# A Strassen-like product for six up-projection groups, channels in quarters, and another order of the seven products

## The chip, the cores and the metric

One core of one Trainium2 chip. The metric is the device time of one execution in microseconds, the median of several runs. The kernel before: 1018.52 us, median of 3 runs (1018.37 to 1019.42).

## The reference

One decoder layer over 512 positions and 1024 channels, in float32: a normalised input goes through one wide projection into four branches (two kinds of linear attention, softmax attention with forgetting, a gated recurrence), which are projected back, weighted by sigmoid gates and summed. Then comes a squared-ReLU channel mixer. The parts that the change touches:

```
z = h @ w_in + b_in                      # its last 4096 columns are the gates
g = sigmoid(gates)
merged = sum(g * (ycat @ w_branch))
x = x + merged @ w_o
h2 = rms_norm(x, norm2_g)                # 512 x 1024
x = x + square(relu(h2 @ w_up)) @ w_down # w_up 1024 x 4096, w_down 4096 x 1024
```

## The kernel before

All large products run on TensorE in float32r with each operand split into a high part (a cast) and a low part (the rest), and three matmuls high·high, high·low and low·high per tile. The unit of work is a `Group` (line 273): 512 output columns of a weight matrix against all 512 positions, four PSUM banks of 512 columns each. With 1024 rows of weights it is 8 x 4 x 3 = 96 matmuls of 512 columns.

Weights come through four raw buffers of 512 KB (line 198), loaded by SP's queue in the order of a plan (`pull`, line 204); a buffer is given back (`give`, line 218) by the step that reads it last, and the next load is issued then. `exact` (line 226) makes a piece out of a raw buffer: ScalarE casts the high part (L229), VectorE subtracts it for the low part (L230). Four such pairs of buffers exist (line 86), so a piece's cast waits until the matmuls of the piece four before it are done. `split(i)` is called three pieces ahead of the product in hand.

`Seven` (line 337) is the other unit. It does the same work as a 96-matmul group by one level of a Strassen-Winograd scheme: the weights are cut into quarters w11, w12, w22, w21 of 512 rows by 256 columns, the input into four quarters, and seven products of half size replace eight. Its pieces p0 to p6 are sums of quarters made by VectorE (the sum of two raw quarters at L360, L364, L368 and L376, then `exact`). Each product is 2 x 4 x 3 = 24 matmuls of 256 columns (L411), 168 in a seven. The products add up in three PSUM banks Y, Z and X; partial sums of Y are copied out by ScalarE between products (L415, in halves, and L419), because later products go on adding in the same bank, and VectorE makes the output quarters (L420, L425, L432). `forms(f)` gives the input's side of a product: a plain quarter or one of four sums, which `combos` (line 1012) makes once, with VectorE and ScalarE. `spare` are two half buffers for the sum that p0 and p4 need.

Of the eight gate groups six are sevens; each is followed by a branch projection, a `Group` of 48 matmuls. The channel mixer does not use `Seven`: two halves of 2048 channels, each four up groups (`up_group`, line 1127; ReLU on ScalarE L1136, square on VectorE L1138, cast on ScalarE L1139, low part on VectorE L1140) and two down groups over these 2048 channels (`down_group`, line 1148; 192 matmuls each, evacuated by VectorE at L1151, which adds into x).

The order of instructions on each engine is made by a scheduler at build time, from the order in the program as priority and from modelled readiness. It also moves instructions between groups: a matmul of the following group can be placed before the last products of a seven. Steps of other work are generators in `gens`, advanced by `pump()` between products.

Of the kernel before, what the change touches and what calls it, by code (L numbers as in the profile page):

```python
# [76 lines left out]
def tile_hybrid(ctx, tc, x, norm1_g, w_in, b_in, ml_norm_g, fx_qnorm_g, fx_knorm_g, lru_conv_w,  # L77
# [37 lines left out]
    def f32(ap):  # L115
        return ap.bitcast(F32)
# [109 lines left out]
    def exact(pc, raw, off=0):  # L226
        halves_tiles(pc, off)
        hi, lo = pc["hl"]
        nc.scalar.copy(hi, raw)  # L229
        nc.vector.tensor_sub(lo, raw, f32(hi))  # L230
# [106 lines left out]
    class Seven:  # L337
# [11 lines left out]
        def plan(self):  # L349
            w11, w12, w22, w21 = lds = [dict(src=s) for s in self.src]  # L350
            loads.extend(lds)
            me = {}

            def take():
                me["e"] = spare[0]
                spare.append(spare.pop(0))
                return me["e"]

            def p0(pc):
                nc.vector.tensor_add(take(), w11["raw"], w12["raw"])  # L360
                exact(pc, w11["raw"], WOFF)

            def p1(pc):
                nc.vector.tensor_add(w11["raw"], me["e"], w22["raw"])  # L364
                exact(pc, me["e"], WOFF)

            def p2(pc):
                nc.vector.tensor_add(w12["raw"], w12["raw"], w22["raw"])  # L368
                exact(pc, w11["raw"], WOFF)

            def p3(pc):
                exact(pc, w12["raw"], WOFF)
                give(w12)

            def p4(pc):
                nc.vector.tensor_add(me["e"], w11["raw"], w21["raw"])  # L376
                exact(pc, w21["raw"], WOFF)
                give(w11, w21)

            def p5(pc):  # L380
                exact(pc, me["e"], WOFF)

            def p6(pc):
                exact(pc, w22["raw"], WOFF)
                give(w22)

            pieces.extend(dict(make=m) for m in (p0, p1, p2, p3, p4, p5, p6))

        def run(self):
            p0 = piece_no[0]  # L390
            piece_no[0] += 7
            Y, Z, X = acc(), acc(), acc()
            y2, z2, x2 = (t.rearrange("p (b c) -> p b c", c=256) for t in (Y, Z, X))
            s1, u2 = w2(), w2()
            seen = set()
            for f, ps in enumerate((Y, Z, Y, Y, X, Y, Z)):
                split(p0 + f + 3)
                whi, wlo = (kview(t, 4) for t in pieces[p0 + f]["hl"])
                ahi, alo = self.forms(f)
                fresh = id(ps) not in seen  # L400
                seen.add(id(ps))
                for b in range(2):
                    o = ps[:, b * 256 : (b + 1) * 256]
                    bs = slice(b * P, (b + 1) * P)
                    for k in range(4):
                        s0 = fresh and b == 0 and k == 0
                        trio = ((whi, ahi), (whi, alo), (wlo, ahi))
                        for n, (w_, a_) in enumerate(trio):
                            fl = dict(start=s0 and n == 0, stop=k == 3 and n == 2, skip_group_check=True)
                            if self.fm:  # L410
                                nc.tensor.matmul(o, w_[:, k, bs], a_[:, k], **fl)  # L411
                            else:
                                nc.tensor.matmul(o, a_[:, k, bs], w_[:, k], **fl)
                    if f in (0, 2):
                        nc.scalar.copy((s1 if f == 0 else u2)[:, b * 256 : (b + 1) * 256], o)  # L415
                    pump()
                if f == 3:
                    d = self.dst(1, 1)
                    nc.scalar.copy(d, y2)  # L419
                    nc.vector.tensor_sub(d, z2, d)  # L420
                    self.post(1, 1, d)
                    pump()
                elif f == 4:
                    d = self.dst(0, 0)
                    nc.vector.tensor_add(d, x2, s1.rearrange("p (b c) -> p b c", c=256))  # L425
                    self.post(0, 0, d)
                elif f == 5:
                    self.post(1, 0, y2)
                    pump()
                elif f == 6:  # L430
                    d = self.dst(0, 1)
                    nc.vector.tensor_sub(d, z2, u2.rearrange("p (b c) -> p b c", c=256))  # L432
                    self.post(0, 1, d)
# [575 lines left out]

    S = {}  # L1010

    def combos(quarter, give_back):

        qs = [slots.get(), slots.get()]
        t11, t12, t21, t22 = (kview(t[:, o : o + 1024], 4) for t in qs for o in (0, 1024))
        for t, (i, j) in ((t21, (1, 0)), (t22, (1, 1)), (t11, (0, 0)), (t12, (0, 1))):
            nc.vector.tensor_add(t, *(f32(a) for a in quarter(i, j)))
# [10 lines left out]
        out(1, t22)  # L1028
        yield
        nc.vector.tensor_sub(t21, t11, t21)  # L1030
        out(3, t21)
        yield
        nc.vector.tensor_sub(t11, t22, t11)
        out(2, t11)
        yield
        nc.vector.tensor_add(t12, t12, t11)
        out(6, t12)
        slots.free(*qs)
        yield

    def h_quarter(i, j):
        return tuple(k4(t[j], 4)[:, :, i * 256 : (i + 1) * 256] for t in (hTh, hTl))

    def h_forms(f):
        return S[f] if f in S else h_quarter(*{0: (0, 0), 4: (0, 1), 5: (1, 1)}[f])

    def gate_seven(n, half):
        def dst(i, j):
# [75 lines left out]

    Rh, Rl = [None] * 4, [None] * 4

    def up_group(g):
        q = g % 4

        def pre():  # L1130
            Rh[q], Rl[q] = slots.get(F32R), slots.get(F32R)
# [13 lines left out]
            lambda k: xgl[k // 4][:, (k % 4) * 512 : (k % 4 + 1) * 512], evac, pre=pre,  # L1145
        )

    def down_group(fh, ch):
        def evac(tb, ps):
            a = xt(tb)[:, ch * 512 : (ch + 1) * 512]  # L1150
            nc.vector.scalar_tensor_tensor(a, ps, r2[:, tb : tb + 1], a, op0=ALU.mult, op1=ALU.add)  # L1151
            if fh == 1:
                nc.scalar.dma_start(out[tb * P : (tb + 1) * P, ch * 512 : (ch + 1) * 512], a)

        return Group(
            w_down[fh * 2048 : (fh + 1) * 2048], ch * 512, 4, False,
            lambda k: Rh[k // 4][:, (k % 4) * 512 : (k % 4 + 1) * 512],
            lambda k: Rl[k // 4][:, (k % 4) * 512 : (k % 4 + 1) * 512], evac,
        )

    ups, downs = [], []
    for fh in range(2):
        ups.append([up_group(fh * 4 + i) for i in range(4)])
        downs.append([down_group(fh, ch) for ch in range(2)])


    plan = [g_fq, g_fk, g_fv, g_gqk, g_gv, g_mq, g_mk, g_gg, g_mv, g_mo, g_rx, g_ry]
    for _, _, a_, b_ in merge_groups:
        plan += [a_, b_]
    plan += og  # L1170
    for fh in range(2):
        plan += ups[fh] + downs[fh]
    for g in plan:
        g.plan()

# [162 lines left out]
    for i, (n, half, gg_, pg_) in enumerate(merge_groups):  # L1338
# [12 lines left out]
            prep(n)  # L1351
        if n == order[-1] and half == 1:
            slots.free(*hTh, *hTl, *s_slots)
        if n == order[0] and half == 1:
            room = slots.get()
            spare.extend((room[:, :1024], room[:, 1024:2048]))
            s_slots.append(room)
# [13 lines left out]
    og[0].run()  # L1371
    og[1].run()
    slots.free(gains, *mh, *ml_)
    for fh in range(2):
        for g in ups[fh]:
            g.run()
        if fh == 0:
            nc.vector.tensor_scalar(r2, r2, 1.0 / D, EPS, op0=ALU.mult, op1=ALU.add)
            nc.vector.reciprocal(r2, r2)
        else:  # L1380
            slots.free(*xgh, *xgl)
        for g in downs[fh]:
            g.run()
        slots.free(*Rh, *Rl)


_INS = ("x", "norm1_g", "w_in", "b_in", "ml_norm_g", "fx_qnorm_g", "fx_knorm_g", "lru_conv_w", "lru_conv_b",
# [22 lines left out]
```

## Time and profile before

| | before |
|---|---|
| median of 3 runs | 1018.52 us |
| the profiled execution | 1018.88 us |
| its span, first to last instruction | 1017.1 us |
| TensorE matmul busy | 1004.4 us (99%) |
| TensorE weight loads busy | 831.2 us (82%) |
| VectorE busy | 561.0 us (55%) |
| ScalarE busy | 414.0 us (41%) |

Matmuls overlap their neighbours in the trace, so the duration of one (about 390 ns for 512 columns) is not its cost; the distance between two starts is. Times in rows of the timeline and the chain count from the span's first instruction.

### The profile page before, as it was taken

To read this page: it belongs to the slowest core of one execution; us is meant where nothing else is said; L and a number is where in the kernel's file an instruction comes from. 1 tells how busy PE (TensorE), PEld (TensorE's weight loads), DVE (VectorE), ACT (ScalarE), POOL (GpSimd) and SP (SyncE) were. 2 spreads that over 40 slices of the span, in tenths; PEclk is the share of its full clock that TensorE was granted. 3 is DMA by queue.
4 is the path that set the end of the run, shared out by engine and by line. 5 is a ranking of instruction groups with operands and counts; after the bars stand their busy time and mean duration, and the time that the engine had idled before them with its cause. 6 is when DMAs were issued, how large, how long until landed. Compare 5 with 4: busy or idle time off the path is not lost.

```text
span 1017.1 us, 12463 instructions
## 1 busy us (share of the span) xinstructions
PE 1004.4 (99%) x4977; PEld 831.2 (82%) x4977; DVE 561.0 (55%) x868; ACT 414.0 (41%) x590; POOL 22.5 (2%) x62
## 2 busy tenths in 40 slices
PE   8999999999999999999999999999999999999998
PEld 5888877877778867889899998888888888888886
DVE  5585454166735969976778765555442224444221
ACT  5352534382544375455454462254432213333120
POOL 2000010000001000000000000000000000000000
PEclk9999999999999999999999999999999999999999
DMA  6634222222322213134232363223332323332321
GB/s 182 208 106 123 63 72 64 83 83 83 104 83 63 71 54 95 51 109 120 84 105 83 109 223 125 83 83 97 111 101 86 104 83 99 108 104 85 115 70 42
DMA packets 60717, 99.60 MB, mean 98 GB/s; under 512 B 8493, under 2 KB 20901, under 8 KB 60402
## 3 DMA queue, kind: packets, MB, share of 16 engines
q1 hardware_dynamic: 58386, 92.76, 30.0%
q10 hardware_dynamic: 1872, 4.72, 1.2%
q0 software_dynamic: 400, 1.31, 0.5%
q8 instruction: 39, 0.64, 0.3%
q14 instruction: 20, 0.16, 0.1%
HBM read 96.66 MB, written 2.11 MB: 97 GB/s over the span
## 4 chain that ended last, share of the span: by engine, by line
PE 95%; ACT 2%; DVE 1%; issue 1%; DMA 1%; SPq 0%; ACTq 0%
PE acc L300 15%; PE acc L301 15%; PE acc L302 15%; PE acc L304 11%; PE acc L306 11%; PE acc L305 11%; PE acc L411 10%; PE sm L733 1%; PE sm L609 1%; PE sm L719 1%; PE sm L636 1%; PE sm L802 1%; DMA s<-in_x_dram 1%; ACT whi L229 1%; PE sm L626 0%
## 5 line engine op out<-in xcount | busy, mean ns | idle before, releaser
L230 DVE TENSOR_TENSOR wlo<-raw,whi 128x1024 fp32r<-128x1024 f32 x172 | 209.8, 1223 | 258.1 <-ACT whi L229 255.3
L229 ACT CAST whi<-raw 128x1024 fp32r<-128x1024 f32 x172 | 179.9, 1048 | 338.3 <-PE acc L306 166.6
L300 PE MATMUL acc<-s,whi 128*128 128x512 f32 x672 | 271.3, 405 | 1.6 <-ACT whi L229 0.9
L302 PE MATMUL acc<-s,wlo 128*128 128x512 f32 x672 | 262.3, 390 | 0.0
L301 PE MATMUL acc<-s,whi 128*128 128x512 f32 x672 | 262.0, 390 | 0.3 <-DVE s L571 0.3
L304 PE MATMUL acc<-whi,s 128*128 128x512 f32 x480 | 191.7, 399 | 0.3 <-ACT s L1220 0.2
L305 PE MATMUL acc<-wlo,s 128*128 128x512 f32 x480 | 187.8, 391 | 0.4 <-DVE wlo L1229 0.4
L306 PE MATMUL acc<-whi,s 128*128 128x512 f32 x480 | 187.8, 391 | 0.0
L300 PEld LDWEIGHTS acc<-s,whi 128*128 128x128 f32 x672 | 126.2, 188 | 31.2 <-issue 2.1
L301 PEld LDWEIGHTS acc<-s,whi 128*128 128x128 f32 x672 | 126.3, 188 | 27.5 <-issue 1.9
L302 PEld LDWEIGHTS acc<-s,wlo 128*128 128x128 f32 x672 | 126.1, 188 | 26.7
L411 PE MATMUL acc<-s,whi 128*128 128x256 f32 x672 | 121.2, 282 | 1.7 <-ACT w L415 1.3
L411 PEld LDWEIGHTS acc<-s,whi 128*128 128x128 f32 x672 | 103.1, 188 | 6.8 <-ACT w L415 4.7
L304 PEld LDWEIGHTS acc<-whi,s 128*128 128x128 f32 x480 | 90.4, 188 | 20.3 <-ACT s L1220 1.2
L306 PEld LDWEIGHTS acc<-whi,s 128*128 128x128 f32 x480 | 90.3, 188 | 20.1 <-DVE s L1221 1.2
L305 PEld LDWEIGHTS acc<-wlo,s 128*128 128x128 f32 x480 | 90.4, 188 | 19.2 <-DVE wlo L1229 1.0
L411 PE MATMUL acc<-s,wlo 128*128 128x256 f32 x336 | 92.7, 279 | 0.0
L411 PEld LDWEIGHTS acc<-s,wlo 128*128 128x128 f32 x336 | 63.1, 188 | 0.0
L1138 DVE TENSOR_TENSOR w<-w 128x512 f32<-128x512 f32 x32 | 22.1, 690 | 21.0 <-ACT w L1136 21.0
L983 ACT ACTIVATE s<-acc,vecs 128x512 f32<-128x512 f32 x28 | 19.1, 685 | 33.8 <-PE acc L302 33.8
L1140 DVE TENSOR_TENSOR s<-w,s 128x512 fp32r<-128x512 f32 x32 | 22.1, 691 | 16.5 <-ACT s L1139 16.5
L1136 ACT ACTIVATE w<-acc 128x512 f32<-128x512 f32 x32 | 19.0, 594 | 27.5 <-PE acc L302 27.5
(235 smaller groups left out, 757.0 us busy)
## 6 DMA issues: line engine op xcount, KB each, us to landing
raw<-in_w_in_dram SPq DMA_DIRECT2D x78, 512.0 KB
raw<-in_w_up_dram SPq DMA_DIRECT2D x32, 512.0 KB
raw<-in_w_down_dram SPq DMA_DIRECT2D x32, 512.0 KB
raw<-in_w_branch_dram SPq DMA_DIRECT2D x16, 512.0 KB
raw<-in_w_o_dram SPq DMA_DIRECT2D x8, 512.0 KB
s<-in_x_dram ACTq DMA_DIRECT2D x4, 512.0 KB
out_dram<-s ACTq DMA_DIRECT2D x8, 256.0 KB
s<-in_x_dram SPq DMA_DIRECT2D x3, 512.0 KB
```

Source lines behind the costliest of these rows:

```text
L229: nc.scalar.copy(hi, raw)
L230: nc.vector.tensor_sub(lo, raw, f32(hi))
L300: nc.tensor.matmul(ps, whi[:, k2, bs], hh, start=s0, stop=False)
L301: nc.tensor.matmul(ps, whi[:, k2, bs], hl, start=False, stop=False)
L302: nc.tensor.matmul(ps, wlo[:, k2, bs], hh, start=False, stop=s1)
L304: nc.tensor.matmul(ps, hh[:, bs], whi[:, k2], start=s0, stop=False)
L305: nc.tensor.matmul(ps, hh[:, bs], wlo[:, k2], start=False, stop=False)
L306: nc.tensor.matmul(ps, hl[:, bs], whi[:, k2], start=False, stop=s1)
L411: nc.tensor.matmul(o, w_[:, k, bs], a_[:, k], **fl)
L983: nc.scalar.activation(cell[0][:, b * width + off : b * width + off + 512], ps, AF.Identity, bias=col(name, base + b))
L1138: nc.vector.tensor_mul(t2, t, t)
L1140: nc.vector.tensor_sub(Rl[q][:, s], t2, f32(Rh[q][:, s]))
```

## The change

The order of a seven's products becomes 0, 1, 2, first half of 3, 4, second half of 3, 5, 6, and what were products 3 and 4 change their numbers with their pieces (p3 is now w21, p4 is w12), so that product 3 goes to bank X. The two partial sums of Y are copied whole, after the product, and no longer in halves. `give` of w12 moves from p3 to p4. Six of the eight up groups become sevens (`up_seven`), with Relu, Square and the cast on ScalarE and the low part on VectorE; their input sums are made by a second use of `combos` while the second up group runs. The channel mixer goes in four quarters of 1024 channels: two up units, then two down groups of 96 matmuls, of which there are eight now. The square of these six moves from VectorE to ScalarE.

```diff
@@ -365,17 +365,16 @@
                 exact(pc, me["e"], WOFF)
 
             def p2(pc):
+                exact(pc, w11["raw"], WOFF)
+
+            def p3(pc):
                 nc.vector.tensor_add(w12["raw"], w12["raw"], w22["raw"])
-                exact(pc, w11["raw"], WOFF)
-
-            def p3(pc):
-                exact(pc, w12["raw"], WOFF)
-                give(w12)
+                exact(pc, w21["raw"], WOFF)
 
             def p4(pc):
                 nc.vector.tensor_add(me["e"], w11["raw"], w21["raw"])
-                exact(pc, w21["raw"], WOFF)
-                give(w11, w21)
+                exact(pc, w12["raw"], WOFF)
+                give(w11, w12, w21)
 
             def p5(pc):
                 exact(pc, me["e"], WOFF)
@@ -392,35 +391,38 @@
             Y, Z, X = acc(), acc(), acc()
             y2, z2, x2 = (t.rearrange("p (b c) -> p b c", c=256) for t in (Y, Z, X))
             s1, u2 = w2(), w2()
-            seen = set()
-            for f, ps in enumerate((Y, Z, Y, Y, X, Y, Z)):
+            both = (0, 1)
+            for f, ps, halves_ in (
+                (0, Y, both), (1, Z, both), (2, Y, both), (3, X, (0,)), (4, Y, both), (3, X, (1,)), (5, Y, both), (6, Z, both)
+            ):
                 split(p0 + f + 3)
                 whi, wlo = (kview(t, 4) for t in pieces[p0 + f]["hl"])
                 ahi, alo = self.forms(f)
-                fresh = id(ps) not in seen
-                seen.add(id(ps))
-                for b in range(2):
+                for b in halves_:
                     o = ps[:, b * 256 : (b + 1) * 256]
                     bs = slice(b * P, (b + 1) * P)
                     for k in range(4):
-                        s0 = fresh and b == 0 and k == 0
                         trio = ((whi, ahi), (whi, alo), (wlo, ahi))
                         for n, (w_, a_) in enumerate(trio):
-                            fl = dict(start=s0 and n == 0, stop=k == 3 and n == 2, skip_group_check=True)
+                            fl = dict(
+                                start=f in (0, 1, 3) and b == 0 and k == 0 and n == 0, stop=k == 3 and n == 2, skip_group_check=True
+                            )
                             if self.fm:
                                 nc.tensor.matmul(o, w_[:, k, bs], a_[:, k], **fl)
                             else:
                                 nc.tensor.matmul(o, a_[:, k, bs], w_[:, k], **fl)
-                    if f in (0, 2):
-                        nc.scalar.copy((s1 if f == 0 else u2)[:, b * 256 : (b + 1) * 256], o)
                     pump()
-                if f == 3:
+                if f == 0:
+                    nc.scalar.copy(s1, Y)
+                elif f == 2:
+                    nc.scalar.copy(u2, Y)
+                elif f == 4:
                     d = self.dst(1, 1)
                     nc.scalar.copy(d, y2)
                     nc.vector.tensor_sub(d, z2, d)
                     self.post(1, 1, d)
                     pump()
-                elif f == 4:
+                elif f == 3 and 1 in halves_:
                     d = self.dst(0, 0)
                     nc.vector.tensor_add(d, x2, s1.rearrange("p (b c) -> p b c", c=256))
                     self.post(0, 0, d)
@@ -1009,9 +1011,9 @@
 
     S = {}
 
-    def combos(quarter, give_back):
-
-        qs = [slots.get(), slots.get()]
+    def combos(quarter, give_back, qs=None):
+
+        qs = qs or [slots.get(), slots.get()]
         t11, t12, t21, t22 = (kview(t[:, o : o + 1024], 4) for t in qs for o in (0, 1024))
         for t, (i, j) in ((t21, (1, 0)), (t22, (1, 1)), (t11, (0, 0)), (t12, (0, 1))):
             nc.vector.tensor_add(t, *(f32(a) for a in quarter(i, j)))
@@ -1028,21 +1030,25 @@
         out(1, t22)
         yield
         nc.vector.tensor_sub(t21, t11, t21)
-        out(3, t21)
+        out(4, t21)
         yield
         nc.vector.tensor_sub(t11, t22, t11)
         out(2, t11)
         yield
         nc.vector.tensor_add(t12, t12, t11)
         out(6, t12)
-        slots.free(*qs)
+        slots.free(qs[0])
+        if not spare:
+            spare.extend((qs[1][:, :1024], qs[1][:, 1024:2048]))
+        else:
+            slots.free(qs[1])
         yield
 
     def h_quarter(i, j):
         return tuple(k4(t[j], 4)[:, :, i * 256 : (i + 1) * 256] for t in (hTh, hTl))
 
     def h_forms(f):
-        return S[f] if f in S else h_quarter(*{0: (0, 0), 4: (0, 1), 5: (1, 1)}[f])
+        return S[f] if f in S else h_quarter(*{0: (0, 0), 3: (0, 1), 5: (1, 1)}[f])
 
     def gate_seven(n, half):
         def dst(i, j):
@@ -1124,8 +1130,14 @@
 
     Rh, Rl = [None] * 4, [None] * 4
 
+    def xg_quarter(i, j):
+        return tuple(k4(t[j], 4)[:, :, i * 256 : (i + 1) * 256] for t in (xgh, xgl))
+
+    def xg_forms(f):
+        return S[f] if f in S else xg_quarter(*{0: (0, 0), 3: (0, 1), 5: (1, 1)}[f])
+
     def up_group(g):
-        q = g % 4
+        q = g % 2
 
         def pre():
             Rh[q], Rl[q] = slots.get(F32R), slots.get(F32R)
@@ -1145,31 +1157,49 @@
             lambda k: xgl[k // 4][:, (k % 4) * 512 : (k % 4 + 1) * 512], evac, pre=pre,
         )
 
-    def down_group(fh, ch):
+    def up_seven(g):
+        q = g % 2
+
+        def dst(i, j):
+            return w2().rearrange("p (b c) -> p b c", c=256)
+
+        def post(i, j, src):
+            if (i, j) == (1, 1):
+                Rh[q], Rl[q] = slots.get(F32R), slots.get(F32R)
+            hi, lo = (k4(t[q], 4)[:, 2 * j : 2 * j + 2, i * 256 : (i + 1) * 256] for t in (Rh, Rl))
+            t = w2().rearrange("p (b c) -> p b c", c=256)
+            nc.scalar.activation(t, src, AF.Relu)
+            nc.scalar.activation(t, t, AF.Square)
+            nc.scalar.copy(hi, t)
+            nc.vector.tensor_sub(lo, t, f32(hi))
+
+        return Seven(w_up, g * 512, True, xg_forms, dst, post)
+
+    def down_group(fq_, ch):
         def evac(tb, ps):
             a = xt(tb)[:, ch * 512 : (ch + 1) * 512]
             nc.vector.scalar_tensor_tensor(a, ps, r2[:, tb : tb + 1], a, op0=ALU.mult, op1=ALU.add)
-            if fh == 1:
+            if fq_ == 3:
                 nc.scalar.dma_start(out[tb * P : (tb + 1) * P, ch * 512 : (ch + 1) * 512], a)
 
         return Group(
-            w_down[fh * 2048 : (fh + 1) * 2048], ch * 512, 4, False,
+            w_down[fq_ * 1024 : (fq_ + 1) * 1024], ch * 512, 2, False,
             lambda k: Rh[k // 4][:, (k % 4) * 512 : (k % 4 + 1) * 512],
             lambda k: Rl[k // 4][:, (k % 4) * 512 : (k % 4 + 1) * 512], evac,
         )
 
     ups, downs = [], []
-    for fh in range(2):
-        ups.append([up_group(fh * 4 + i) for i in range(4)])
-        downs.append([down_group(fh, ch) for ch in range(2)])
+    for fq_ in range(4):
+        ups.append([(up_seven if fq_ else up_group)(fq_ * 2 + i) for i in range(2)])
+        downs.append([down_group(fq_, ch) for ch in range(2)])
 
 
     plan = [g_fq, g_fk, g_fv, g_gqk, g_gv, g_mq, g_mk, g_gg, g_mv, g_mo, g_rx, g_ry]
     for _, _, a_, b_ in merge_groups:
         plan += [a_, b_]
     plan += og
-    for fh in range(2):
-        plan += ups[fh] + downs[fh]
+    for fq_ in range(4):
+        plan += ups[fq_] + downs[fq_]
     for g in plan:
         g.plan()
 
@@ -1351,6 +1381,7 @@
             prep(n)
         if n == order[-1] and half == 1:
             slots.free(*hTh, *hTl, *s_slots)
+            spare.clear()
         if n == order[0] and half == 1:
             room = slots.get()
             spare.extend((room[:, :1024], room[:, 1024:2048]))
@@ -1371,17 +1402,25 @@
     og[0].run()
     og[1].run()
     slots.free(gains, *mh, *ml_)
-    for fh in range(2):
-        for g in ups[fh]:
+    s_slots = []
+    for fq_ in range(4):
+        for g in ups[fq_]:
             g.run()
-        if fh == 0:
+            if g is ups[0][0]:
+                while gens:
+                    pump()
+                g_sums = combos(xg_quarter, s_slots)
+                gens.append(g_sums)
+            elif g is ups[0][1]:
+                drain(g_sums)
+        if fq_ == 0:
             nc.vector.tensor_scalar(r2, r2, 1.0 / D, EPS, op0=ALU.mult, op1=ALU.add)
             nc.vector.reciprocal(r2, r2)
-        else:
-            slots.free(*xgh, *xgl)
-        for g in downs[fh]:
+        elif fq_ == 3:
+            slots.free(*xgh, *xgl, *s_slots)
+        for g in downs[fq_]:
             g.run()
-        slots.free(*Rh, *Rl)
+        slots.free(*Rh[:2], *Rl[:2])
 
 
 _INS = ("x", "norm1_g", "w_in", "b_in", "ml_norm_g", "fx_qnorm_g", "fx_knorm_g", "lru_conv_w", "lru_conv_b",
```

## Rows read from the trace of the kernel before

**Rows 1.** The page: busy time, clock in 40 slices, chain by engine.

```profile
PE 1004.4 (99%) x4977; PEld 831.2 (82%) x4977; DVE 561.0 (55%) x868; ACT 414.0 (41%) x590; POOL 22.5 (2%) x62
...
PEclk9999999999999999999999999999999999999999
...
PE 95%; ACT 2%; DVE 1%; issue 1%; DMA 1%; SPq 0%; ACTq 0%
```

**Rows 2.** Windows (length, busy by engine): six gate sevens' sum, one, projection, four up groups.

```profile
sum 128.38, PE 125.78 PEld 120.17 DVE 84.47 ACT 78.08 POOL 0.00; mean PE 20.96 PEld 20.03 DVE 14.08 ACT 13.01 POOL 0.00
...
459.08:479.95 20.87, 20.82 (x171) 19.87 (x170) 12.06 (x13) 11.43 (x18) 0.00 (x0) 1.00 0.41 116
480.00:490.60 10.60, 10.60 (x49) 8.52 (x47) 10.05 (x12) 3.02 (x4) 0.00 (x0) 1.00 0.22 68
839.12:926.16 87.04, 87.04 (x386) 72.07 (x384) 39.67 (x47) 33.85 (x46) 0.00 (x0) 1.00 0.32 97
```

**Rows 3.** Timeline, TensorE, two stretches: start, duration, line; a pair starts six matmuls apart.

```profile
438.92 0.28 PE L411 MATMUL acc<-s,wlo 128*128 128x256 f32 x1
...
439.63 0.28 PE L411 MATMUL acc<-s,wlo 128*128 128x256 f32 x1
...
444.89 0.28 PE L411 MATMUL acc<-s,wlo 128*128 128x256 f32 x1
...
445.57 0.28 PE L411 MATMUL acc<-s,wlo 128*128 128x256 f32 x1
```

**Rows 4.** Chain of waits in one seven: start, duration, what.

```profile
468.58 0.80 issue
469.37 0.37 ACT w L415
...
469.79 4.16 PE acc L411 x33
473.94 0.47 PE acc L300
474.41 0.23 PE acc L301
```

**Rows 5.** Timeline of ScalarE at the same place; in brackets idle time before.

```profile
468.42 1.05 ACT L229 CAST whi<-raw 128x1024 fp32r<-128x1024 f32 x1 [1.62 <-PE acc L411]
469.37 0.36 ACT L415 COPY w<-acc 128x256 f32<-128x256 f32 x1
```

**Rows 6.** Waits of TensorE's weight loads: us in total, times, longest.

```profile
PEld acc L411 <- ACT w L415: 4.7, 16, 1.2
```

**Rows 7.** Groups by line and form: busy us, mean ns, idle before and releaser.

```profile
L230 DVE TENSOR_TENSOR wlo<-raw,whi 128x1024 fp32r<-128x1024 f32 x172 | 209.8, 1223 | 258.1 <-ACT whi L229 255.3 <-PE sm L908 1.4 <-PE sm L802 0.8
L229 ACT CAST whi<-raw 128x1024 fp32r<-128x1024 f32 x172 | 179.9, 1048 | 338.3 <-PE acc L306 166.6 <-PE acc L301 121.0 <-PE acc L411 32.4
...
L1140 DVE TENSOR_TENSOR s<-w,s 128x512 fp32r<-128x512 f32 x32 | 22.1, 691 | 16.5 <-ACT s L1139 16.5
...
L1139 ACT CAST s<-w 128x512 fp32r<-128x512 f32 x32 | 19.8, 619 | 25.5 <-DVE w L1138 25.5
...
L1136 ACT ACTIVATE w<-acc 128x512 f32<-128x512 f32 x32 | 19.0, 594 | 27.5 <-PE acc L302 27.5
...
L1151 DVE SCALAR_TENSOR_TENSOR s<-acc,r,s 128x512 f32<-128x512 f32 x16 | 12.0, 749 | 30.3 <-PE acc L306 30.3
...
L360 DVE TENSOR_TENSOR s<-raw,raw 128x1024 f32<-128x1024 f32 x6 | 7.3, 1218 | 0.0
...
L425 DVE TENSOR_TENSOR s<-acc,w 128x512 f32<-128x512 f32 x6 | 4.1, 684 | 5.6 <-PE acc L411 5.6
...
L419 ACT COPY s<-acc 128x512 f32<-128x512 f32 x6 | 3.5, 579 | 0.0
```

**Rows 8.** Timeline of VectorE: the first sum that needs w22.

```profile
479.29 1.23 DVE L368 TENSOR_TENSOR raw<-raw,raw 128x1024 f32<-128x1024 f32 x1 [0.71 <-DMA raw<-in_w_in_dram]
```

**Rows 9.** Timeline of SP's queue: the issues of w22 and w21.

```profile
475.14 2.70 SPq L212 DMA_DIRECT2D raw<-in_w_in_dram  x2
```

More of the change, by code (lines that the diff above doesn't have):

```diff
@@ L367, in p2 @@
             def p2(pc):
-                nc.vector.tensor_add(w12["raw"], w12["raw"], w22["raw"])
                 exact(pc, w11["raw"], WOFF)
             def p3(pc):
-                exact(pc, w12["raw"], WOFF)
-                give(w12)
+                nc.vector.tensor_add(w12["raw"], w12["raw"], w22["raw"])
+                exact(pc, w21["raw"], WOFF)
             def p4(pc):
                 nc.vector.tensor_add(me["e"], w11["raw"], w21["raw"])
-                exact(pc, w21["raw"], WOFF)
-                give(w11, w21)
+                exact(pc, w12["raw"], WOFF)
+                give(w11, w12, w21)
             def p5(pc):
```

## The prediction

> **What bounds the kernel now.** I read the page first: TensorE is busy 99% of the span, the chain that ended last is 95% TensorE, and the granted clock is full in all 40 slices, which is the 2.4 GHz level [rows 1]. So the time is the number of matmuls times the distance from one start to the next, plus a few stalls, and the question is what the change does to these three.
>
> The windows come next [rows 2]. Four up-projection groups take 87.04 us, 21.76 each; a group is 96 matmuls of 512 columns, so 226.7 ns apart with no stall at all. The six gate sevens take 128.38 us. A seven is 168 matmuls of 256 columns, but the scheduler has drawn one to three matmuls of the next projection into each (two of them, L300 and L301, in the chain of [rows 4]; 1, 2, 2, 2, 2 and 3 in order of the sevens). These 12 cost 12 x 0.2267 = 2.72, which leaves 125.66 us, 20.94 a seven.
>
> The timeline shows two spacings of the half-size matmuls: six starts in 0.68 us (113.3 ns, half of 226.7) in one stretch and six in 0.71 us (118 ns) in another [rows 3]. Of 960 undisturbed gaps 468 were of the first kind and 492 of the second; after each stall it can be either, and every seven begins in the slower one. The mean is about 115.6, and 1008 x 0.1156 = 116.5 us. The other 9.1 us, 1.5 a seven, is stall.
>
> What stalls is in the chain and in ScalarE's timeline. A cast (L229) waits until matmuls free its weight buffer and runs 1.05 us; the copy of the bank (L415) stands behind it in ScalarE's order; the next product is to add into that same bank and starts when the copy has ended, at 469.79 [rows 4, 5]. TensorE's weight loads wait 4.7 us in 16 waits for L415 alone [rows 6]. Products 0, 2, 3 and 5 share the bank Y and follow each other closely, so each copy of Y is exposed.
>
> **The order of products (twelve sevens).** The new order is 0 (Y), 1 (Z), 2 (Y), 3 first half (X), 4 (Y), 3 second half (X), 5 (Y), 6 (Z). After product 0 the copy of 0.58 us [rows 7] has product 1, 24 x 0.116 = 2.8 us, as cover. After product 2 it has half a product, 12 x 0.116 = 1.39 us. If the cast is ahead of it as in [rows 5], the copy ends 1.05 + 0.58 = 1.63 us after the product, so 0.25 us stays exposed. Behind the waiting matmul on TensorE stands only the rest of the seven. After product 4 the copy has 1.39 us and no cast that was freed with it, because the next cast needs product 3's buffer. The read after product 5 has product 6. I take 0.5 us of stall for a seven: 0.25 worked out and as much for late casts and for the first seven, which comes out of the preparation of a branch. The ends are 0 and today's 1.5. With fewer stalls more of a seven runs at the 118 it begins with, so I take 116.5 ns: 168 x 0.1165 + 0.5 = 20.07. Gates: 125.66 - 6 x 20.07 = 5.2 us saved; ends 125.66 - 1008 x 0.1133 = 11.5 saved and 1008 x 0.118 + 9.1 - 125.66 = 2.4 lost.
>
> **Six up-projection groups as sevens.** Each was 21.76 us without a stall [rows 2] and becomes 20.07, so 1.69 x 6 = 10.1 us saved. The ends: 168 x 0.1133 = 19.03 saves 16.4; 168 x 0.118 + 1.5 = 21.32 saves 2.6.
>
> The page "TensorE: Matmul & The Clock Gate" of the Trainium skill (section "Wait — 56ns, not 53.3ns?") speaks against small matmuls: besides a column per cycle each pays about 2.5 ns. By it a group would be 96 x 215.8 = 20.7 us and a seven 168 x 109.2 = 18.3, an estimate that saves 2.4 each, 14.3 in six. The rows disagree with both figures: 226.7 and 113.3 are exact halves, with no fixed part, and the slower state adds 4.7.
>
> **VectorE and ScalarE in these sevens.** VectorE: four sums of raw weights at 1.22, seven second halves at 1.22, three additions from banks at 0.68, four second halves of the result at 0.69: 4.9 + 8.6 + 2.1 + 2.8 = 18.3 us [rows 7]. ScalarE: seven casts at 1.05, three copies at 0.58, and four times Relu, Square and cast at about 0.6 (the Square, which no row here shows at this size, taken like the other two): 7.3 + 1.7 + 7.3 = 16.4. TensorE needs 19.6, so VectorE is 93% full. Two such sevens follow each other in a quarter. I still count this at nothing: splits stand three products ahead (some 8 us), the last three of each pair lie in the down group behind it, and VectorE already runs 10.05 of 10.60 us in a projection without TensorE losing any (10.60 busy) [rows 2]. If that cover goes, rival C prices it.
>
> **The sums of the normalised input.** The new combos makes four sums, three differences and one sum, and four casts with second halves: 12 x 1.22 = 14.6 us of VectorE and 4 x 1.05 = 4.2 of ScalarE. It is pumped in the second up group, where VectorE has four second halves, four squares and four halves: 4.9 + 5.5 = 10.4. Together 25.0 in 21.76, so 3.3 us run over, into a down group where VectorE has 4.9 + 4 x 0.75 = 7.9 us in 21.76 [rows 7]. TensorE needs the second group's result only in the second half of that down group, 10.9 us after its start, and its banks are freed by ScalarE. Cost 0, at worst 3.3.
>
> **Buffers and loads.** Piece 3's weight buffer is held until the second half of product 3, and the piece four later, the next group's first, can be cast only then; products 5 and 6 still lie ahead, 5.6 us, for 1.05 + 1.22. The raw quarter w12 comes back one piece later, so the load of the next group's second quarter starts about 2.8 us later on SP's queue, and those behind it too. A load issued at 475.14 was in use at 479.29 after a wait of 0.71 [rows 8, 9], so some 4 us. In a pair that puts w12 at about 5 + 4 and w22 behind it at about 11, before its first sum at about 14. Cost 0. The piece ahead of the first seven of a quarter is one fewer, since a group splits two pieces ahead at its end; its third is needed 5.6 us into the seven and takes 2.3.
>
> **Down projection in quarters.** 768 matmuls of 512 columns as before; 32 evacuations for 16 add 16 x 0.75 = 12 us of VectorE, which is in the 7.9 of 21.76 above. Cost 0. The last group, its evacuation and the outputs are unchanged.
>
> **Sum.** The profiled execution took 1018.88 us (span 1017.1, 1.8 around it), 0.4 over the median of 1018.52. 5.2 + 10.1 = 15.3, less 0.5 for what runs over: 1018.88 - 14.8 = 1004.1; I say 1004.
>
> **Rivals.**
> A. The order hides nothing: the scheduler puts casts ahead of the copies again and stalls stay at 1.5. For it: it already lets a copy wait for a cast that comes free with it. Against: two of the three copies have cover longer than 1.63 or no cast before them. Gates save 0, an up seven is 19.57 + 1.5 = 21.07 and saves 0.69, 4.1 in all: 1014.7.
> B. No stall stays and the spacing settles at 113.3: 11.5 + 16.4 = 27.9, so 991; with half of that luck, 997. For it: stretches of over 40 matmuls at that spacing. Against: each seven begins at 118.
> C. Slower: the second seven of a pair is bound by the in-order exchange of VectorE and ScalarE. Eleven times a seven, one waits for the other (seven casts, 7.3 us, and four chains of three, 7.3 us). If half of these 14.7 us lies bare, VectorE needs 18.3 + 7.3 = 25.6 us, 3.8 more than the old group; at six that is 23, less 5.2 at the gates: 1037. It decides from 21.76 + 5.2/6 = 22.6 us a seven, 4.3 us of bare waits. For it: VectorE's 93%, and the waits of the up groups now, where L1140 and L1139 wait for each other [rows 7]. Against: the scheduler finds other work in between, as in the 10.05 of 10.60.
>
> **How the numbers follow.** Forecast 0.60 (its own range 998 to 1011), A 0.16 (1010 to 1020), B 0.14, C 0.10 (half of it milder, 1010 to 1020). The range 995 to 1015 leaves out the best half of B, the worst of A and most of C. About 0.2% (2 us) is what a measurement can tell. Faster: 0.60 + three quarters of A + B + a little of C = 0.88; same 0.04; slower 0.08.
>
> **What would show it.** Right: the gate sevens fall from 20.94 to about 20 us, the wait for L415 to under 1.5 us; six up stretches of about 20 us; no wait of TensorE for VectorE in the quarters. Wrong: sevens of over 21.8 us in the quarters, with matmuls waiting for whi or wlo; a gap in the first down group; copies of a bank still on the chain after product 0 or 4; a chain in which TensorE has less than 95%.

## The result and the profile after

The kernel after takes 1002.86 us, median of 4 runs (1001.29 to 1003.85), against 1018.44 (1018.35 to 1019.42) for the kernel before: ratio 0.9843, 95% interval 0.9826 to 0.986. The forecast was 1004 us. The profiled execution took 1001.29 us, span 999.6, so 17.6 us less than that of before, 2 more than the medians differ.

Those 2 us lie ahead of the change: in some runs the granted clock falls for a moment at about 69 us, with TensorE busy on both sides of it, and the compared executions of before and after are not among them. Windows of the same 20 us, first in the profile of before, then in another profile of after (length; busy of PE, PEld, DVE, ACT, POOL, each with its instructions; granted clock; DMA share; GB/s):

```profile
60.00:80.00 20.00, 20.00 (x102) 16.66 (x102) 19.78 (x47) 8.56 (x13) 0.54 (x1) 1.00 0.44 138
```
```profile
60.00:80.00 20.00, 20.00 (x96) 16.46 (x95) 19.05 (x46) 8.92 (x13) 0.54 (x1) 0.91 0.34 120
```

A mean of 0.91 says that a part of these 20 us was granted at the lower level, 1.2 GHz: 6 matmuls fewer, and the first gate seven starts 2.25 us later (at 428.46 us, for 426.21 in the compared execution of after).

The page after (busy by engine; chain by engine), against [rows 1]:

```profile
PE 989.1 (99%) x5409; PEld 839.3 (84%) x5409; DVE 628.1 (63%) x932; ACT 453.8 (45%) x642; POOL 22.5 (2%) x62
...
PE 96%; ACT 1%; DVE 1%; DMA 1%; issue 0%; SPq 0%
```

432 matmuls more (six units of 168 for 96), and still 15 us less TensorE time; the bound is the same engine.

Windows after: the sum over the six gate sevens, then the two plain up groups but for their first 18 matmuls, then the three pairs of up sevens, against [rows 2]:

```profile
sum 121.05, PE 121.03 PEld 118.43 DVE 84.16 ACT 76.54 POOL 0.00; mean PE 20.17 PEld 19.74 DVE 14.03 ACT 12.76 POOL 0.00
...
662.90:702.44 39.54, 39.54 (x177) 32.74 (x176) 28.26 (x34) 19.61 (x26) 0.00 (x0) 1.00 0.29 94
745.96:785.87 39.91, 39.87 (x339) 39.02 (x337) 29.28 (x30) 26.62 (x38) 0.00 (x0) 1.00 0.41 129
829.19:869.09 39.90, 39.86 (x338) 39.01 (x337) 29.28 (x30) 26.61 (x38) 0.00 (x0) 1.00 0.43 129
912.41:952.32 39.91, 39.87 (x338) 39.02 (x337) 29.18 (x30) 26.62 (x38) 0.00 (x0) 1.00 0.42 129
```

The six gate stretches hold 6 matmuls of the next projection, 1.36 us, which leaves 119.69, 19.95 a seven, for 20.94 before. The pairs, less one matmul of the down group behind each, take 119.04 us, 19.84 a seven, for the old group's 21.76. The plain up stretch has 174 matmuls in 39.54 us, 227.3 ns apart: no stall. The input sums lie in it, but not in its second group, as was reckoned: the scheduler drew them forward, and VectorE's last instruction for them ends at 680.86 us, where the second group has just begun (680.68):

```profile
679.64 1.22 DVE L1027 TENSOR_TENSOR s<-s,s 128x1024 fp32r<-128x1024 f32 x1
```

What stall is left shows in the chain of waits in one gate seven (start, duration, what), in ScalarE's timeline there, and in the weight loads' waits over the whole span (us in total, times, longest; first after, then one more line of before):

```profile
457.28 14.24 PE acc L411 x120
471.51 0.28 PE acc L300
471.79 5.69 PE acc L411 x48
```
```profile
465.68 1.05 ACT L229 CAST whi<-raw 128x1024 fp32r<-128x1024 f32 x1 [1.74 <-PE acc L411]
466.63 0.58 ACT L418 COPY w<-acc 128x512 f32<-128x512 f32 x1
...
470.19 1.05 ACT L229 CAST whi<-raw 128x1024 fp32r<-128x1024 f32 x1 [2.98 <-PE acc L411]
471.14 0.58 ACT L421 COPY s<-acc 128x512 f32<-128x512 f32 x1
```
```profile
PEld acc L411 <- ACT w L418: 2.2, 11, 0.2
...
PEld acc L411 <- ACT s L421: 1.7, 6, 0.3
PEld acc L411 <- ACT w L421: 1.4, 6, 0.3
```
```profile
PEld acc L411 <- ACT s L419: 1.0, 5, 0.3
```

For the copy after product 0 no wait is left. For the one after product 2 (L418) the loads wait 2.2 us over twelve sevens, 0.9 of it at the six gates, where the copies in halves had cost 4.7 in 16 waits [rows 6]. The copy after product 4 (L421, into s at the gates, into w in the pairs) is waited for in every seven, 1.7 us at the gates, where its counterpart before (L419) had 1.0. Each copy still stands directly behind a cast that matmuls have just freed, as in [rows 5], but now a half product covers most of the two. The copy L421 after product 4 has a cast ahead of it too; at the gates the scheduler put one matmul of the next projection (L300) into the gap.

### The profile page after: what moved, and what is told of

Its sections match the earlier page's. It is cut to its first block, busy times and chain, and to the rows that moved or that the text cites. A ratio compares the mean times of both kernels' runs of the same rounds, so it can differ in the third digit from the quotient of the medians.

```text
span 999.6 us, 13471 instructions
## 1 busy us (share of the span) xinstructions
PE 989.1 (99%) x5409; PEld 839.3 (84%) x5409; DVE 628.1 (63%) x932; ACT 453.8 (45%) x642; POOL 22.5 (2%) x62
## 4 chain that ended last, share of the span: by engine, by line
PE 96%; ACT 1%; DVE 1%; DMA 1%; issue 0%; SPq 0%
PE acc L411 24%; PE acc L304 11%; PE acc L306 11%; PE acc L305 11%; PE acc L301 10%; PE acc L302 10%; PE acc L300 10%; PE sm L735 1%; PE sm L721 1%; PE sm L611 1%; PE sm L638 1%; PE sm L804 1%; DMA s<-in_x_dram 1%; PE sm L628 0%; PE sm L1105 0%; PE sm L939 0%
## 5 line engine op out<-in xcount | busy, mean ns | idle before, releaser
L230 DVE TENSOR_TENSOR wlo<-raw,whi 128x1024 fp32r<-128x1024 f32 x178 | 217.0, 1222 | 168.3 <-ACT whi L229 165.6
L411 PE MATMUL acc<-s,whi 128*128 128x256 f32 x1344 | 237.7, 280 | 0.1
L411 PEld LDWEIGHTS acc<-s,whi 128*128 128x128 f32 x1344 | 205.7, 189 | 6.0 <-ACT w L418 2.2
L300 PE MATMUL acc<-s,whi 128*128 128x512 f32 x480 | 196.1, 410 | 0.7 <-ACT s L572 0.7
L301 PE MATMUL acc<-s,whi 128*128 128x512 f32 x480 | 187.3, 390 | 0.3 <-DVE s L573 0.3
L302 PE MATMUL acc<-s,wlo 128*128 128x512 f32 x480 | 187.5, 391 | 0.0
L411 PE MATMUL acc<-s,wlo 128*128 128x256 f32 x672 | 185.9, 278 | 0.0
L411 PEld LDWEIGHTS acc<-s,wlo 128*128 128x128 f32 x672 | 125.9, 188 | 0.0
L300 PEld LDWEIGHTS acc<-s,whi 128*128 128x128 f32 x480 | 90.1, 188 | 21.5 <-issue 2.1
L301 PEld LDWEIGHTS acc<-s,whi 128*128 128x128 f32 x480 | 90.3, 188 | 20.2 <-issue 1.9
L302 PEld LDWEIGHTS acc<-s,wlo 128*128 128x128 f32 x480 | 90.1, 188 | 19.0
L1181 DVE SCALAR_TENSOR_TENSOR s<-acc,r,s 128x512 f32<-128x512 f32 x32 | 23.9, 748 | 40.2 <-PE acc L306 40.2
L230 DVE TENSOR_TENSOR wlo<-s,whi 128x1024 fp32r<-128x1024 f32 x24 | 29.3, 1221 | 17.9 <-ACT whi L229 17.9
L229 ACT CAST whi<-s 128x1024 fp32r<-128x1024 f32 x24 | 25.2, 1049 | 26.7 <-PE acc L306 13.3
```

The costliest lines, as they stand in the source:

```text
L300: nc.tensor.matmul(ps, whi[:, k2, bs], hh, start=s0, stop=False)
L301: nc.tensor.matmul(ps, whi[:, k2, bs], hl, start=False, stop=False)
L302: nc.tensor.matmul(ps, wlo[:, k2, bs], hh, start=False, stop=s1)
```

## Experiments

**The order alone** (kernel before, with the new order, numbering and whole copies in the gate sevens, no up sevens; the line that sets the order):

```diff
...
-            for f, ps in enumerate((Y, Z, Y, Y, X, Y, Z)):
+            for f, ps, halves_ in (
+                (0, Y, both), (1, Z, both), (2, Y, both), (3, X, (0,)), (4, Y, both), (3, X, (1,)), (5, Y, both), (6, Z, both)
+            ):
...
```

> The kernel before with the new order of products in the six gate sevens alone, the channel mixer untouched. Theory (the order takes the stalls of the bank copies out of the gate sevens, the up groups gain apart from it): the six stretches fall from 128.4 to about 122.4 us, the time by 5 to 6.5 us, to 1012 to 1013.5. Rival (the two parts need each other, for example because the gain comes from the quarters): under 3 us. In the trace: about 0.25 us of stall after product 2 in each seven, none after 0 and 4, and 84 matmuls at 118 ns from each start.

Measured: 1013.71 us against 1018.37, ratio 0.9944 (0.9931 to 0.9958). Its sum over the six gate stretches:

```profile
sum 122.02, PE 122.00 PEld 119.41 DVE 85.24 ACT 76.73 POOL 0.00; mean PE 20.33 PEld 19.90 DVE 14.21 ACT 12.79 POOL 0.00
```

Less 6 drawn-in matmuls that is 120.66, 5.0 under before. The gate term stands by itself.

**The sevens alone** (kernel after, with the old order and the two copies in halves in every seven; the diff above reversed):

> The changed kernel (quarters, six up sevens, their input sums) with the order of products and the copies of before in all twelve sevens. Theory: the gate sevens are as before (128.4 us in six stretches), each up seven stands at about 20.9 us in place of 21.76, so 5 us less than before in all: 1013.5, and 10 to 12 us over the changed kernel. Rival (in the pairs ScalarE is fuller, so that copies wait longer behind casts and ReLUs): the up sevens reach 21.8 or more and nothing is left of the gain, 1018 or more. Rival the other way (the order is worth little in the pairs): under 1009.

Measured: 1018.59 us, ratio 0.9991 (0.9981 to 1.0001). Six sevens without the order bring next to nothing; by the windows it is 1.8 us (the pairs less three drawn-in matmuls are 128.80 us, for 130.56 of six up groups). Windows of its three pairs, the two sevens of the first, the weight loads' wait in it, and ScalarE inside it:

```profile
754.14:797.44 43.30, 41.86 (x339) 39.60 (x337) 29.28 (x30) 27.45 (x43) 0.00 (x0) 1.00 0.37 120
840.75:883.85 43.10, 41.66 (x339) 39.39 (x337) 29.28 (x30) 27.24 (x42) 0.00 (x0) 1.00 0.38 119
927.17:970.25 43.08, 41.64 (x339) 39.38 (x337) 29.18 (x30) 27.24 (x42) 0.00 (x0) 1.00 0.38 119
```
```profile
754.14:774.70 20.56, 20.50 (x169) 19.52 (x168) 14.77 (x15) 11.87 (x18) 0.00 (x0) 1.00 0.33 103
774.70:797.44 22.74, 21.36 (x172) 20.08 (x170) 14.51 (x16) 15.57 (x26) 0.00 (x0) 1.00 0.41 136
```
```profile
PEld acc L411 <- ACT w L415: 2.6, 7, 1.1
```
```profile
777.15 1.04 ACT L229 CAST whi<-raw 128x1024 fp32r<-128x1024 f32 x1
778.09 0.62 ACT L1170 ACTIVATE w<-w 128x512 f32<-128x512 f32 x1
778.62 0.35 ACT L415 COPY w<-acc 128x256 f32<-128x256 f32 x1
```

The pairs sum to 129.48 us for 119.72 after: the order is worth 9.8 us here, and with the gates (125.36 us for 119.69, drawn-in matmuls taken off) nearly the whole change. The second seven of a pair is the dear one: ahead of its copy stands not only a cast but an activation of the seven before (L1170), which no gate seven has directly ahead of it. In all these runs "the order" is the new order, the numbering and the whole copies together; what the whole copies are worth by themselves was not measured.

**The u2 copy on VectorE**, where no cast is ahead of it:

```diff
-                    nc.scalar.copy(u2, Y)
+                    nc.vector.tensor_copy(u2, Y)
```

> The changed kernel, the copy of Y after product 2 on VectorE in place of ScalarE, in all twelve sevens, so that it stands behind no cast. Theory of stalls: the last regular stall, 0.37 us with its restart, goes, 12 x 0.37 = 4.4 us less, about 998. Rival, theory of spacing (matmuls of 256 columns that follow 512-column ones without a stall stay 118 ns apart, and any short stall brings them to 113.3): the stall goes, but the 84 matmuls behind it stay at 118, 84 x 0.0045 = 0.38 us a seven lost, so no change within 1 us in the nine sevens that begin slow, and at most 1 us gained in the three others.

Measured: 1008.1 us, ratio 0.989 (0.9874 to 0.9905), about 5 us slower than after. At the gates the second to the fifth seven are 19.71 us, drawn-in matmul taken off, for about 19.98 in after: the stall of 0.25 us after product 2 is gone, and the 120 starts up to the stall after product 4 stay 117.8 ns apart. (The first took 20.77 for 20.00, for a reason that was not looked into; the last had no such stall in after either.) The loss is in the pairs; the second one's window, the weight loads' waits over the three, and VectorE at the place:

```profile
831.38:874.22 42.84, 39.72 (x338) 38.90 (x337) 30.57 (x32) 25.65 (x36) 0.00 (x0) 1.00 0.38 121
```
```profile
PEld acc L411 <- DVE w L418: 6.8, 3, 3.3
```
```profile
843.01 1.23 DVE L360 TENSOR_TENSOR s<-raw,raw 128x1024 f32<-128x1024 f32 x1 [3.55 <-DMA raw<-in_w_up_dram]
844.16 0.68 DVE L418 COPY w<-acc 128x512 f32<-128x512 f32 x1
```

The second seven's first sum waits 3.55 us for a load of w_up, and the copy stands behind it on VectorE. In the kernel after the same sum waits too, with nothing behind it that TensorE waits for (VectorE's waits over its three pairs):

```profile
DVE s L360 <- DMA raw<-in_w_up_dram: 7.1, 3, 2.7
```

Neither theory had this: the loads are late, and cost nothing only while the queue behind them is free.

**The spacing: a short matmul ahead of every seven.** Six starts take 0.68 or 0.71 us [rows 3]; does a matmul of 64 columns, whose result the first product overwrites, choose which?

```diff
+                if f == 0:
+                    nc.tensor.matmul(Y[:, :64], whi[:, 0, :P], ahi[:, 0, :64], start=True, stop=True, skip_group_check=True)
```

> The changed kernel with one more matmul of 64 columns in front of each seven, into bank Y, where the first product overwrites it. Theory of spacing by phase (what width ran before sets it): the 84 matmuls from a start run at 113.3 ns, 0.38 us a seven in nine sevens less 0.03 to 0.1 for the added matmul in twelve, so 2 to 3 us less than the changed kernel, about 1000. Rival (the spacing at a start comes from something else, such as what ScalarE and VectorE do there): still 118 ns, and up to 1.2 us slower for the added matmuls.

Measured: 1002.81 us, 0.9837 (0.982 to 0.9854), where after has 0.9843 and, run again, 0.9844: no gain. Yet the first three and a half products are faster; windows of that stretch in this kernel and in after, of the product's line alone (84 matmuls and the start of one more; the first window begins with the short one):

```profile
458.77:468.41 9.64, 9.61 (x85) 9.64 (x85) 1.00 0.35 109
```
```profile
457.11:467.01 9.90, 9.90 (x85) 9.89 (x84) 1.00 0.35 106
```

9.90 us are 117.8 ns each; here the short one and a restart behind it take 0.23 us, and the 83 starts that follow 9.41 us, 113.4 ns each. But the stall after product 2 is longer here (0.31 us from start to start, for 0.25), and behind the one after product 4 the last 47 matmuls of this seven are 117.7 ns apart, for 113.3 in after. A gain in spacing can only be counted on where no stall follows.

**No stall: casts behind the copies.** The casts of p6 and of p7, the next unit's first piece, are put behind the two copies in ScalarE's order:

```diff
-                split(p0 + f + 3)
+                if f == 3 and 0 in halves_:
+                    with tc.issue_after(cp.ins):
+                        split(p0 + 6)
+                elif f != 4:
+                    split(p0 + f + 3)
...
-                    nc.scalar.copy(d, y2)
+                    cp = nc.scalar.copy(d, y2)
+                    with tc.issue_after(cp.ins):
+                        split(p0 + 7)
```

> The changed kernel with the copies of Y after products 2 and 4 queued ahead of the casts that come free with them on ScalarE. Theory of spacing (without a stall the matmuls of a seven stay 118 ns apart): the regular stalls go, and all 168 matmuls of a seven run at 117.8, 19.8 us in place of 20.0 at the gates and 19.84 in the pairs; 0 to 2 us less than the changed kernel. Rival (a stall costs its own length and nothing else): 0.57 us a seven, 5 to 7 us less.

Measured: 1001.69 us, 0.9823 (0.9805 to 0.984), 1.7 less than the run of after beside it. One gate seven and one pair, and ScalarE at the u2 copy:

```profile
428.10:447.89 19.79, 19.79 (x169) 19.78 (x168) 17.06 (x18) 15.75 (x23) 0.00 (x0) 1.00 0.40 116
746.90:786.47 39.57, 39.57 (x338) 39.57 (x336) 28.75 (x30) 26.85 (x40) 0.00 (x0) 1.00 0.38 124
```
```profile
467.48 0.59 ACT L422 COPY w<-acc 128x512 f32<-128x512 f32 x1 [1.85 <-PE acc L415]
467.96 1.05 ACT L229 CAST whi<-raw 128x1024 fp32r<-128x1024 f32 x1
```

The copy is first, TensorE's busy time is the whole window, and every seven takes 168 x 117.8 ns = 19.79 us. The stalls are gone, and only 1.7 us with them, because now nothing breaks the slower spacing: 336 matmuls in a row have it.

**Both together** (the diffs of the short matmul and of the casts):

> As the kernel with copies first, and with the 64-column matmul in front of each seven. Theory of spacing: all 168 run at 113.3 ns, 19.04 + 0.12 = 19.16 us a seven, 0.8 us less at the gates and 0.7 in the pairs, 8 to 10 us less than the changed kernel, about 994. Rival (the spacing falls back to 118 within the seven without any stall): 0 to 3 us less.

Measured: 997.29 us, 0.9784 (0.977 to 0.9798), 6.1 less than the run of after beside it, for the 8 to 10 expected. A gate seven, two pairs, and the chain in a gate seven:

```profile
425.93:445.06 19.13, 19.13 (x171) 19.13 (x169) 17.06 (x18) 15.64 (x23) 0.00 (x0) 1.00 0.41 121
740.95:781.28 40.33, 39.33 (x339) 39.12 (x338) 28.76 (x30) 26.86 (x40) 0.00 (x0) 1.00 0.38 122
824.83:863.89 39.06, 39.06 (x340) 39.06 (x338) 28.75 (x30) 26.88 (x40) 0.00 (x0) 1.00 0.40 127
```
```profile
456.12 0.03 PE acc L406
456.15 19.13 PE acc L417 x168
```

After the short one (L406) come 168 matmuls without a break at 113.3 ns, but in a pair the second short matmul turns the spacing back: 19.13 and then 19.87 us. The first pair has a stall of 1.27 us besides, with a bank's copy behind the evacuations of the seven before.

**Where the short matmul stands.** Both kernels have the casts behind the copies. The first has the short matmul ahead of every seven but the second of a pair, the other, as the reverse, only there (`last[0]` names the unit before):

```diff
...
-                if f == 0:
+                if f == 0 and last[0] != 'seven':
...
```
```diff
...
-                if f == 0:
+                if f == 0 and last[0] == 'seven':
...
```

> Copies first, and the 64-column matmul only where a seven follows a group of 512-column matmuls: the six gate sevens and the first of each pair. Theory of spacing (the short matmul changes the state of the stream, from 118 to 113.3 in front of the first of a pair, but from 113.3 back to 118 in front of the second, as the run with nine more of them showed): both sevens of a pair at 113.3, pairs of 38.2 to 39.5 us in place of 39.0 to 40.3, 2.5 to 3.7 us less than with a short matmul everywhere: 993.5 to 995. Rival (with TensorE faster, ScalarE at the change from the first to the second seven becomes the bound): stalls of 1 to 2 us in each pair, no gain, 997 or more.

> Copies first, and the 64-column matmul only in front of the second seven of a pair, which without it runs at 118 behind a first seven at 118. If a short matmul shifts the stream from either state into the other: second sevens at 113.3, 0.75 us less in each of three, about 999.5 (2 us under the kernel with copies first and no short matmul, 1001.7). If the state is set by the short matmul's own place (always 118 between two sevens): no change within 0.5 us, 1001.7.

Measured: the first 994.2 us against 1020.37, 0.9752 (0.9737 to 0.9766), the best version here, 26.2 us under the runs of before beside it and under every run of after; the second 999.86, 0.9794 (0.9778 to 0.9809). A gate seven and the three pairs of the first, then the two sevens of a pair of the second:

```profile
427.95:447.11 19.16, 19.16 (x170) 19.16 (x169) 17.06 (x18) 15.67 (x23) 0.00 (x0) 1.00 0.41 120
742.98:781.82 38.84, 38.49 (x338) 38.29 (x337) 28.55 (x30) 26.60 (x40) 0.00 (x0) 1.00 0.39 124
825.37:863.57 38.20, 38.20 (x339) 38.20 (x337) 28.55 (x30) 26.64 (x40) 0.00 (x0) 1.00 0.39 127
907.11:945.32 38.21, 38.21 (x339) 38.20 (x337) 28.56 (x30) 26.69 (x40) 0.00 (x0) 1.00 0.40 127
```
```profile
746.69:766.48 19.79, 19.79 (x170) 19.79 (x168) 14.94 (x15) 11.97 (x18) 0.00 (x0) 1.00 0.35 107
766.48:785.65 19.17, 19.17 (x171) 19.17 (x170) 13.61 (x16) 14.63 (x23) 0.00 (x0) 1.00 0.42 145
```

With the stalls gone the short matmul turns the spacing over wherever it stands: 117.8 to 113.3 in the second kernel's pair, and back in the kernel that has one ahead of every seven. With stalls it need not: in the pairs of the kernel with the short matmul alone, the scheduler drew the second one into the stall after product 4 of the first seven, and the spacing is 113.3 ns before and behind it. In the first of the two kernels here the first pair keeps one gap of 0.63 us, again with a bank's copy on ScalarE late.

**Rival C: the Square back on VectorE** (kernel after, in `up_seven`):

```diff
-            nc.scalar.activation(t, t, AF.Square)
+            nc.vector.tensor_mul(t, t, t)
```

> The changed kernel with the Square of the up sevens on VectorE, as the plain up groups have it: VectorE 18.3 + 2.8 = 21.1 us for a seven of 19.84, ScalarE 16.4 - 2.5 = 13.9. It puts the cover of VectorE to the test. Theory (VectorE is near its limit in a pair, only the splits that fall into the down groups keep it hidden): a pair grows by 1 to 4 us, the time by 3 to 12. Rival (ScalarE, which has no gap for 14 us at the change from the first seven to the second, is the tighter of the two): no change within 1.5 us, or a little less.

Measured: 1005.05 us, 0.9862 (0.9847 to 0.9876), 1.7 over the run of after beside it. Two pairs:

```profile
748.91:789.34 40.43, 40.43 (x338) 39.58 (x337) 31.52 (x35) 24.01 (x32) 0.00 (x0) 1.00 0.39 126
832.66:872.72 40.06, 40.02 (x338) 39.09 (x337) 31.53 (x35) 24.04 (x32) 0.00 (x0) 1.00 0.40 129
```

VectorE is at 31.5 of 40.4 us and TensorE doesn't wait for it: over the three pairs the weight loads wait only for the two copies, 2.5 us, as in after (2.6). What the first of them loses is 129 matmuls at 117.8 ns. C was not near.

**The kernel after once more**, beside three of these (casts behind the copies, both together, the Square):

> The changed kernel once more, beside the three others of this set and for more runs: 1002 to 1004 us. In some runs the clock falls to its lower level for a few us at about 69 us, which is worth up to 2 us; runs with and without it should both turn up here.

Measured: 1003.39 us, 0.9844 (0.9828 to 0.9861). The sum over the six gate stretches of its profile:

```profile
sum 122.04, PE 122.02 PEld 119.42 DVE 85.56 ACT 76.73 POOL 0.00; mean PE 20.34 PEld 19.90 DVE 14.26 ACT 12.79 POOL 0.00
```

The same kernel had 121.05. In five of the six sevens the 47 matmuls behind the stall after product 4 are 117.7 ns apart here and 113.3 there. So the gates save 5.0 us in this execution, as with the order alone, and 6.0 in the other: the program does not fix which spacing follows a stall.

## Why the prediction was right

| Term | predicted, us | measured in the profiled executions, us |
|---|---|---|
| six gate sevens | 5.2 saved (ends -2.4 and 11.5) | 125.66 - 119.69 = 5.97 saved (4.98 in the second execution) |
| six up groups as sevens | 10.1 saved (2.6 to 16.4) | 130.56 - 119.04 = 11.52 saved |
| sums run over | 0.5 lost | 0 (227.3 ns in the stretch; the sums end with the first group) |
| down groups, loads | 0 | 17.6 - 17.5 = 0.1 |

The mechanism is the one forecast, and shown from both sides: the order alone saves 5.0 us at the gates, and without it the up sevens save 1.8 in place of 11.5. The stall of 0.25 us after product 2 came out as worked out. That the median lies so near 1004 is luck in part: the sum counts from an execution of 1018.88 us, and the one to compare with it took 1001.29, so the terms missed 2.7 us.

Five things were wrong, and they cancelled or stayed hidden:

- "After product 4 the copy has 1.39 us and no cast that was freed with it, because the next cast needs product 3's buffer." The cast of 470.19 took the buffer that product 4 had just left, and the copy ran behind it to 471.72. This stall, about 0.3 us in eleven of the twelve sevens, took a little more than the 0.25 that had been set aside for late casts.
- The spacing, 116.5 ns taken for all: in the compared execution mostly 84 matmuls at 117.8 and, behind the stall, 84 at 113.3, 115.6 in the mean, and 113.3 for nearly all of a pair's second seven. 168 x 0.9 ns = 0.15 us in eight sevens and 168 x 3.2 ns = 0.5 in three are some 2.8 us; the stalls took about 0.6 more than was set aside. With the next point this is the 2.7 that the sum missed (17.5 for 14.8).
- "It is pumped in the second up group", and 3.3 us run over. The scheduler made the sums earlier, the last by 680.86 us, and nothing ran over: the 0.5 lost was not lost.
- Rival A's price. A seven in the old order was put at 21.07 us in the quarters, as at the gates, so that without the order 0.69 us a seven would stay. It measured 21.47 (129.48 less three drawn-in matmuls, over six), by the second seven of each pair (22.5 us in the first pair, for 20.6 in its first seven), whose copy stands behind the evacuations of the seven before on ScalarE too. The forecast was right to give the order most weight, but had the order failed, the time would have been 1018.6 and not 1014.7.
- "VectorE is 93% full." It is busy 29.28 of 39.91 us, 73%. The splits of the pair's end fall into the next group, and instructions that follow each other start earlier than the durations say (last section). ScalarE, counted lighter at 16.4 us, is busy 26.62 us in a pair, and it is ScalarE's order that decided every stall of TensorE in the sevens of the kernel after.

"Cost 0" for the loads held for another reason than the one given: they are up to 2.7 us late for the second seven's first sum, and it is only the products still ahead of that sum's piece that keep TensorE from waiting.

## What to carry to other kernels

When an in-order engine has to read a bank before the next product may write it, put other matmuls between them, and count what stands ahead of the read in that engine's order, evacuations of the unit before included: here that was worth 15.4 us by the windows, about as much as the arithmetic of six sevens saves at best (16.4). When the stalls are gone, measure the distance between starts as well; it held another 7.5 us of 1002 (1001.69 to 994.2). And a wait costs nothing only as long as nothing on the path is queued behind it: moving one copy to the idler engine cost 5 us.

## What the runs showed of the hardware

Matmuls of 256 columns run at one of two steady spacings, 113.3 and 117.8 ns, at the same granted clock of 1.00. A seven behind a 512-column group starts with the second and keeps it to the end if nothing interrupts it; a stall, or one matmul of 64 columns, can turn either into the other, and behind a stall the same kernel had 113.3 in one execution and 117.7 in another. "TensorE: Matmul & The Clock Gate" in the Trainium skill (section "Back-to-back issue gap") gives one figure for an isolated matmul of 256 columns, 262 cycles, by which an estimate is 109 ns; no run here shows it, and the two that they show decide. What holds the two apart was not settled: the runs show what turns them, not why.

Instructions of one engine overlap in the records: a VectorE sum of 1.23 us is followed 1.15 us after its start (843.01 and 844.16 above), a ScalarE cast of 1.05 us after 0.95 (465.68 and 466.63, 470.19 and 471.14). Sums of durations so overstate how full an engine is.
